# Differential attention scores: the low pass of q on half the array's rows, and both components of a query block scored in one step

## The chip, the cores and the metric

The kernel runs on one core of a Trainium2 chip. The metric is the device time of one execution in microseconds (us), lower is better; the time before is the median of three runs.

The core has a matrix engine (TensorE, PE; its weight loads are listed apart as PEld), a vector engine (VectorE, DVE), an engine for activations and copies (ScalarE, ACT), a general engine (GpSimd, POOL), and SyncE (SP), which issues the DMAs here. Each works through its own queue in order; semaphores join them. Matmul results land in PSUM.

## The reference

Two layers on 1024 tokens of width 1024: a pooling mixer and a gated MLP, then differential attention and a gated MLP. Attention has 8 heads; each has two components of 64 dimensions. Cut to what matters:

```python
def _diff_attention(x, w_qkv, ..., cos, sin, layer_idx):
    q, k, v = jnp.split(x @ w_qkv, 3, axis=-1)
    q = _rope(...).reshape(b, s, h, 2, dh) * (dh ** -0.5)      # h = 8 heads, 2 components, dh = 64
    k = _rope(...).reshape(b, s, h, 2, dh)
    v = v.reshape(b, s, h, 2 * dh)
    ...
    def one_block(qb):                                          # 128 queries
        sc = jnp.einsum('bqhce,bkhce->bhcqk', qb, k)
        p = jax.nn.softmax(sc, axis=-1)
        a = p[:, :, 0] - lam * p[:, :, 1]                       # component 0 minus lam times component 1
        return jnp.einsum('bhqk,bkhe->bqhe', a, v)
    o = lax.map(one_block, q_blocks)
    ...
    return _rms_norm(o, subln) * (1.0 - lam_init) @ w_o
```

All is float32 in the reference.

## The kernel before

Matmuls take 32-bit operands that are rounded. To keep precision, an operand is split into a high part (the rounded value) and a low part (what is left), and a product is computed as a sum of two or three matmuls.

**Layout of the scores.** The contraction of one component is 64 long, half of the 128 rows of the array. The tile `kst[:, c]` holds, for component c, the high part of k in rows 64c to 64c+63 (`own`) and its low part in the other 64 rows. q stands twice, in both halves: `qhi` is its high part, `qlo` its low part. So a matmul of `qhi[:, c]` with `kst[:, c]` over all 128 rows gives q_high x k_high + q_high x k_low, and the pass with `qlo[:, c]` gives q_low x k_high + q_low x k_low. A query block has 128 queries and 1024 keys, hence two matmuls of 512 columns for each pass and component.

**A query block**, 8 to a head, 64 in all. `score_q` makes `qhi` on ACT and `qlo` on POOL. `score_mm` runs the four matmuls of one component into a PSUM tile `sc` of 1024 columns (there are two such tiles), then DVE takes the row maximum (`nm`, L1108), for component 0 it subtracts a constant (L1110), and ACT takes the exponential and its row sum (L1111). `combine` (DVE, L1117 to L1122) forms component 0 minus the scaled component 1 in place, in two halves of the keys. `a_prep` transposes one half of the keys on PE (`aT`, L1137), and splits the result into `a_hi` (ACT) and `a_lo` (DVE, line 132 in a helper). `pv` multiplies two blocks at a time with v (`po`, L1148, 24 matmuls of 256 columns). `o_turn` transposes the output; `finish_*` normalizes a head.

**The order on PE** is written by hand: under `manual_schedule` PE executes in the order of the code, and the code is emitted by walking a string for each block, in turn the first and the second of `PLAN` (`PLAN7` in the last head). Each character is a step: `s` scores component 0 of this block, `S` component 1, `a` and `b` transpose the two halves of the block before, `q` is `score_q` of the next block, `c` is `combine`, `p` is `pv`, `t` is `o_turn`, and `.` takes the next step of `filler`: two matmuls of the projections of the next head (`pj`, L1020 and L1062), later of the output projection. On DVE, ACT and POOL the scheduler of the framework orders instructions by priority and by when it believes them ready.

Of the kernel before, what the change touches and what calls it, by code (L numbers as in the profile page):

```python
# [11 lines left out]
F32 = mybir.dt.float32  # L12
F32R = mybir.dt.float32r
I32 = mybir.dt.int32
AF = mybir.ActivationFunctionType
ALU = mybir.AluOpType
AX = mybir.AxisListType
# [3 lines left out]
P = 128  # L21
S = 1024
# [3 lines left out]
NT = S // P  # L26
NK = D // P
ORDER = (0, 4, 1, 5, 2, 6, 3, 7)
PLAN = ("...saq.bS..c.p", "st.aS.m.q.fb....F.c..")
PLAN7 = (".as.b....S.pqc.", "tmsaSqcb..f......F..")  # L30
AHEAD = 3
WQ, RQ = 14, 3
PB = (2, 1)
# [56 lines left out]
def trunk_kernel(  # L90
# [24 lines left out]
    V, A, PE = nc.vector, nc.scalar, nc.tensor  # L115

    def pool(es, name, bufs=1, space=None, side=None):
        kw = {}
        if space is not None:
            kw["space"] = space  # L120
        if side is not None:
            kw["side"] = side
        if space is not DRAM:
            kw["reuse_waits"] = "tile"
        return es.enter_context(tc.tile_pool(name=name, bufs=bufs, **kw))
# [824 lines left out]
    p_p = pool(at_es, "pp", bufs=2)  # L950
    a_p = pool(at_es, "ap", bufs=1)
    o_p = pool(at_es, "op", bufs=1)
    ps_sc = pool(at_es, "ps_sc", bufs=2, space=PSUM)
# [6 lines left out]
    for src, dst in ((cosT, cosF), (sinT, sinF)):  # L960
        wide = p_p.tile([P, NT, 4, 32], F32, name="prob0")
        V.tensor_copy(wide, src.unsqueeze(2).broadcast_to([P, NT, 4, 32]))
        for q in range(2):
# [3 lines left out]
            cols = slice(512 * q, 512 * q + 512)  # L967
# [109 lines left out]
    soft, sums = {}, {}  # L1077

    scored = {}

    def score_q(j, i):
        with tc.high_priority(offset=20):
            tq = qt[j, i // 2] if i % 2 == 0 else qt.pop((j, i // 2))
            src = tq[:, :, (i % 2) * P:(i % 2 + 1) * P]
            qhi = p_p.tile([P, 2, P], F32R, name="q_hi")
            qlo = p_p.tile([P, 2, P], F32R, name="q_lo")
            A.copy(qhi, src)  # L1087
            nc.gpsimd.tensor_tensor(qlo, src, f32(qhi), ALU.subtract)  # L1088
            scored[j, i] = qhi, qlo

    def score_mm(j, i, c):
        with tc.high_priority(offset=20):
            ks = kst[j]
            qhi, qlo = scored[j, i]
            if i == 0 and c == 0:
                sums[j] = p_p.tile([P, 2, NT], F32, name="sums")
            sm = sums[j]
            if c == 0:
                soft[j, i] = []
            soft[j, i].append(p_p.tile([P, S], F32, name=f"prob{c}", bufs=PB[c]))  # L1100
            if True:
                sc = ps_sc.tile([P, S], F32, name="sc")
                for l in (qhi, qlo):
                    for n in range(2):
                        ns_ = slice(n * 512, (n + 1) * 512)
                        PE.matmul(sc[:, ns_], l[:, c], ks[:, c, ns_], start=(l is qhi), stop=(l is qlo))  # L1106
                nm = small.tile([P, 1], F32, name=f"nm{c}")
                V.tensor_reduce(nm, sc, AX.X, ALU.max, negate=True)  # L1108
                if c == 0:
                    V.tensor_scalar(nm, nm, -10.0 * math.log(2.0), None, ALU.add)  # L1110
                A.activation(soft[j, i][c], sc, AF.Exp, bias=nm, accum_out=sm[:, c, i:i + 1])  # L1111

    def combine(j, i):
        with tc.high_priority(offset=50):
            (p0, p1), sm = soft[j, i], sums[j]
            r1 = small.tile([P, 1], F32, name="r1")
            V.reciprocal(r1, sm[:, 1, i:i + 1])  # L1117
            cc = small.tile([P, 1], F32, name="cc")
            V.scalar_tensor_tensor(cc, sm[:, 0, i:i + 1], neglam, r1, ALU.mult, ALU.mult)
            for q in range(2):  # L1120
                hq = slice(512 * q, 512 * q + 512)
                V.scalar_tensor_tensor(p0[:, hq], p1[:, hq], cc, p0[:, hq], ALU.mult, ALU.add)  # L1122
# [5 lines left out]
    def a_prep(j, i, q):  # L1128
        with tc.high_priority(offset=20):
            if i % 2 == 0 and q == 0:  # L1130
                at[j, i // 2] = (a_p.tile([P, NT, 256], F32R, name="a_hi"), a_p.tile([P, NT, 256], F32R, name="a_lo"))
            ahi, alo = at[j, i // 2]
            a = soft[j, i][0] if q == 0 else soft.pop((j, i))[0]
            pt = ps_tr.tile([P, 4, P], F32, name="aT", tag="tr")
            for k in range(4):
                kt = 4 * q + k
                PE.transpose(pt[:, k], a[:, kt * P:(kt + 1) * P], ident)  # L1137
            dsl = (slice(None), slice(4 * q, 4 * q + 4), slice((i % 2) * P, (i % 2 + 1) * P))
            split(pt, ahi[dsl], alo[dsl])

    def pv(j, pair):
        vhi, vlo = vst[j]
        ahi, alo = at.pop((j, pair))
        po = ps_tr.tile([P, 256], F32, name="po", tag="tr")
        n = 0
        for k in range(NT):
            for l, r in ((vhi, ahi), (vhi, alo), (vlo, ahi)):
                PE.matmul(po, l[:, k], r[:, k], start=(n == 0), stop=(n == 3 * NT - 1))  # L1148
                n += 1
        pos[j, pair] = po  # L1150
# [133 lines left out]

    assert sum(p.count('.') for p in PLAN) == 18
    done = []
# [4 lines left out]
    with tc.manual_schedule(engines={mybir.EngineType.PE}):  # L1291
        for g in range(H * NT + 2):
            j, i = divmod(g, NT)
            pj, pi = divmod(g - 1, NT)
            for step in (PLAN7 if j == H - 1 else PLAN)[g % 2]:
                if step == ".":
                    if j < H:
                        next(fill, None)
                elif step in "sS":
                    if j < H:  # L1300
                        score_mm(j, i, "sS".index(step))
                elif step == "q":
                    if g + 1 < H * NT:
                        score_q(*divmod(g + 1, NT))
                elif step == "c":
                    if j < H:
                        combine(j, i)
                elif step in "ab":
                    if 0 < g <= H * NT:
                        a_prep(pj, pi, "ab".index(step))  # L1310
                elif step == "p":
                    if 0 < g <= H * NT:
                        pv(pj, pi // 2)
                elif step == "t":
                    if g > 2:
                        hj, hi_ = divmod(g - 2, NT)
                        o_turn(hj, hi_ // 2)
                        if hi_ == NT - 1:
                            finish_a(hj)
                elif step == "m":  # L1320
                    if i == 3 and j:
                        finish_m(j - 1)
                        done.append(j)
                elif step in "fF":
                    if i == 3 and j:
                        finish_b(j - 1, "fF".index(step))
                        done.append(j)
# [85 lines left out]
```

## Time and profile before

| | |
|---|---|
| median of 3 runs | 2119.53 us (2117.35 to 2125.2) |
| profiled execution | 2117.11 us, span of its instructions 2115.3 us |
| mean granted TensorE clock | 0.98 |
| busy: PE / DVE / ACT / POOL | 2015.5 / 1558.6 / 1020.1 / 899.8 us |
| scores: first to last matmul | 803.9 to 1369.5 us of the span |
| score matmuls (512 columns) | 256 high and 256 low |
| row maxima on DVE, L1108 | 128, 155.7 us |
| exponentials on ACT, L1111 | 128, 142.7 us |

Times of instructions are from one profiled execution. An engine's busy time counts the stretches in which it had an instruction in hand; PE's matmul records overlap, so their durations do not add up. A row of the trace reads: start, duration, engine, line, operation, output <- inputs, shape, count.

### The profile page before, as it was taken

What the parts mean: (1) busy time and instruction counts of PE and PEld (TensorE: products, weight loads), DVE (VectorE), ACT (ScalarE), POOL (GpSimd) and SP (SyncE); (2) the same over time, 40 slices, a digit from 0 to 9 for tenths busy, and PEclk for the clock granted to TensorE, in tenths of its full rate; (3) what the DMA queues carried; (4) which work ended last, traced back from release to release, by engine and by line L of the source; (5) the groups of instructions that cost most, each with busy time, mean ns of one, the idle gap of its engine ahead of it and who ended that gap; (6) DMA issues with size and microseconds to landing.
All of it is one profiled execution on the core that took longest, in us unless ns stands there. A gap on an engine that the chain in (4) does not pass through costs nothing.

```text
span 2115.3 us, 27608 instructions
## 1 busy us (share of the span) xinstructions
PE 2015.5 (95%) x9659; PEld 1669.5 (79%) x9659; DVE 1558.6 (74%) x2278; ACT 1020.1 (48%) x1830; POOL 899.8 (43%) x689
## 2 busy tenths in 40 slices
PE   6789999999999799999999998987999999999997
PEld 5678888888888677888888887876888888888885
DVE  7867777777584648899889987767667777774646
ACT  7643333333453545676667666555433333344433
POOL 4599999995000000101110111024999999920000
PEclk8899999999999999999999999998999999999999
DMA  4225454554965412122212216253346445467653
GB/s 168 95 84 181 138 190 138 158 177 144 375 211 174 163 54 67 48 72 62 61 46 73 57 40 224 90 189 110 120 144 198 146 161 167 139 227 278 205 201 130
DMA packets 221720, 301.90 MB, mean 143 GB/s; under 512 B 17852, under 2 KB 142092, under 8 KB 218764
## 3 DMA queue, kind: packets, MB, share of 16 engines
q1 hardware_dynamic: 221580, 300.13, 43.4%
q8 instruction: 76, 1.25, 0.2%
q14 instruction: 64, 0.52, 0.1%
HBM read 196.78 MB, written 90.70 MB: 136 GB/s over the span
## 4 chain that ended last, share of the span: by engine, by line
PE 82%; DVE 9%; ACT 3%; DMA 3%; issue 2%; SPq 1%; POOL 0%; DVEq 0%; ACTq 0%; POOLq 0%
PE dn L597 17%; PE up_b L422 16%; PE up_c L422 11%; PE up_a L422 11%; PE pj L1020 6%; PE sc L1106 4%; PE pj L1062 4%; PE po L1148 3%; PE aT L1137 2%; PE pj L1233 2%; DVE nm L1108 1%; PE pp L844 1%; PE pl L824 1%; ACT hnT_hi L580 1%; DVE hnT_lo L581 1%
## 5 line engine op out<-in xcount | busy, mean ns | idle before, releaser
L1088 POOL TENSOR_TENSOR q_lo<-qt,q_hi 128x256 fp32r<-128x256 f32 x64 | 49.7, 777 | 698.3 <-ACT q_hi L1087 616.8
L380 POOL TENSOR_TENSOR w_lo<-s,w_hi 128x512 fp32r<-128x512 f32 x168 | 274.2, 1632 | 17.7 <-ACT w_hi L379 17.2
L597 PE MATMUL dn<-hnT_hi 128*128 128x512 f32 x584 | 229.7, 393 | 12.0 <-ACT hnT_hi L580 11.8
L597 PE MATMUL dn<-hnT_lo,hnT_hi 128*128 128x512 f32 x584 | 230.2, 394 | 4.4 <-DVE hnT_lo L581 4.4
L597 PE MATMUL dn<-hnT_hi,hnT_lo 128*128 128x512 f32 x584 | 228.8, 392 | 0.0
L422 PE MATMUL up_b<-x_hi,w_hi 128*128 128x512 f32 x528 | 207.2, 392 | 5.3 <-ACT x_hi L304 4.4
L422 PE MATMUL up_b<-x_lo,w_hi 128*128 128x512 f32 x528 | 206.6, 391 | 2.3 <-DVE x_lo L305 2.3
L380 POOL TENSOR_TENSOR w_lo<-raw,w_hi 128x512 fp32r<-128x512 f32 x130 | 195.3, 1503 | 30.6 <-ACT w_hi L379 26.4
L422 PE MATMUL up_b<-x_hi,w_lo 128*128 128x512 f32 x528 | 206.2, 391 | 0.0
L379 ACT CAST w_hi<-s 128x512 fp32r<-128x512 f32 x176 | 108.4, 616 | 178.9 <-PE up_b L422 87.4
L1108 DVE TENSOR_REDUCE nm<-sc 128x1 f32<-128x1024 f32 x128 | 155.7, 1216 | 15.4 <-PE sc L1106 14.6
L1111 ACT ACTIVATE prob<-sc,nm 128x1024 f32<-128x1024 f32 x128 | 142.7, 1115 | 22.3 <-DVE nm L1108 11.7
L422 PE MATMUL up_a<-hnT_hi,w_hi 128*128 128x512 f32 x352 | 139.3, 396 | 1.4 <-ACT g L499 0.9
L597 PEld LDWEIGHTS dn<-hnT_hi 128*128 128x128 f32 x584 | 110.5, 189 | 37.1 <-ACT hnT_hi L580 13.5
L422 PE MATMUL up_a<-hnT_lo,w_hi 128*128 128x512 f32 x352 | 138.9, 395 | 0.1
L422 PE MATMUL up_a<-hnT_hi,w_lo 128*128 128x512 f32 x352 | 138.5, 394 | 0.0
L394 POOL TENSOR_TENSOR s<-raw 128x512 f32<-128x512 f32 x84 | 133.1, 1584 | 10.3 <-DMA raw<-in_ffn_w_up_dram 4.1
L422 PE MATMUL up_c<-hnT_hi,w_lo 128*128 128x512 f32 x352 | 137.0, 389 | 0.2 <-DVE w_lo L380 0.2
L422 PE MATMUL up_c<-hnT_hi,w_hi 128*128 128x512 f32 x352 | 136.9, 389 | 0.0
L422 PE MATMUL up_c<-hnT_lo,w_hi 128*128 128x512 f32 x352 | 136.9, 389 | 0.0
L581 DVE TENSOR_TENSOR hnT_lo<-mst,hnT_hi 128x1024 fp32r<-128x1024 f32 (+1 forms) x80 | 90.2, 1127 | 61.3 <-ACT hnT_hi L580 61.1
L597 PEld LDWEIGHTS dn<-hnT_lo,hnT_hi 128*128 128x128 f32 x584 | 110.5, 189 | 31.0 <-DVE hnT_lo L581 8.4
(298 smaller groups left out, 5362.6 us busy)
## 6 DMA issues: line engine op xcount, KB each, us to landing
raw<-in_ffn_w_up_dram SPq DMA_DIRECT2D x88, 512.0 KB, 4.3
mst<-m_dram SPq DMA_DIRECT2D x70, 512.0 KB, 5.8
wd<-in_ffn_w_down_dram SPq DMA_DIRECT2D x22, 1024.0 KB, 6.0
wd_dram<-wd SPq DMA_DIRECT2D x22, 1024.0 KB, 6.4
m_dram<-cm SPq DMA_DIRECT2D x80, 256.0 KB, 5.6
wst<-wd_dram SPq DMA_DIRECT2D x40, 512.0 KB, 4.8
m_dram<-gc SPq DMA_DIRECT2D x66, 256.0 KB, 6.3
wst<-in_ffn_w_down_dram SPq DMA_DIRECT2D x30, 512.0 KB, 6.1
```

The costliest lines, as they stand in the source:

```text
L379: A.copy(hi, src)
L380: eng.tensor_tensor(lo, src, f32(hi), ALU.subtract)
L394: eng.tensor_tensor(t, a, b, op)
L422: PE.matmul(acc, l[a][:, k], r[b][:, k], start=first and n == 0, stop=n == 11, skip_group_check=True)
L581: V.tensor_tensor(l_, x, f32(h_), ALU.subtract)
L597: PE.matmul(banks[t], l[:, q, cols], r[:, q], start=first and cnt == 0, stop=stop and cnt == 3 * n - 1, skip_group_check=True)
L1020: PE.matmul(acc, l[:, k % 2, h], r[:, k], start=(n == 0), stop=(n == 3 * NK - 1))
L1062: PE.matmul(acc, l[:, k % 4], r[:, k], start=(n == 0), stop=(n == 3 * NK - 1))
L1106: PE.matmul(sc[:, ns_], l[:, c], ks[:, c, ns_], start=(l is qhi), stop=(l is qlo))
L1108: V.tensor_reduce(nm, sc, AX.X, ALU.max, negate=True)
L1111: A.activation(soft[j, i][c], sc, AF.Exp, bias=nm, accum_out=sm[:, c, i:i + 1])
L1148: PE.matmul(po, l[:, k], r[:, k], start=(n == 0), stop=(n == 3 * NT - 1))
```

## The change

`score_mm` now scores both components of a block at the step `s`; the step `S` is gone from the strings, in which nothing else changes. The four high matmuls (two for each component) come first, over 128 rows as before. Then the four low ones, each over only the 64 rows in which k's high part of its component stands: rows 0 to 63 for component 0, rows 64 to 127 for component 1, in turn, so that two neighbours lie on different halves of the array and write to different score tiles. The product q_low x k_low is no longer formed. The row maxima, the exponentials, their tiles and buffers are as before.

```diff
-PLAN = ("...saq.bS..c.p", "st.aS.m.q.fb....F.c..")
+PLAN = ("...saq.b..c.p", "st.a.m.q.fb....F.c..")
...
-    def score_mm(j, i, c):
+    def score_mm(j, i):
         with tc.high_priority(offset=20):
             ks = kst[j]
-            qhi, qlo = scored[j, i]
-            if i == 0 and c == 0:
+            qhi, qlo = scored.pop((j, i))
+            if i == 0:
                 sums[j] = p_p.tile([P, 2, NT], F32, name="sums")
             sm = sums[j]
-            if c == 0:
-                soft[j, i] = []
-            soft[j, i].append(p_p.tile([P, S], F32, name=f"prob{c}", bufs=PB[c]))
-            if True:
-                sc = ps_sc.tile([P, S], F32, name="sc")
-                for l in (qhi, qlo):
-                    for n in range(2):
-                        ns_ = slice(n * 512, (n + 1) * 512)
-                        PE.matmul(sc[:, ns_], l[:, c], ks[:, c, ns_], start=(l is qhi), stop=(l is qlo))
+            soft[j, i] = [p_p.tile([P, S], F32, name=f"prob{c}", bufs=PB[c]) for c in range(2)]
+            scs = [ps_sc.tile([P, S], F32, name="sc") for _ in range(2)]
+            cols = [slice(n * 512, (n + 1) * 512) for n in range(2)]
+            for c in range(2):
+                for ns_ in cols:
+                    PE.matmul(scs[c][:, ns_], qhi[:, c], ks[:, c, ns_], start=True, stop=False)
+            for ns_ in cols:
+                for c in range(2):
+                    own = slice(64 * c, 64 * c + 64)
+                    PE.matmul(scs[c][:, ns_], qlo[own, c], ks[own, c, ns_], start=False, stop=True)
+            for c in range(2):
                 nm = small.tile([P, 1], F32, name=f"nm{c}")
-                V.tensor_reduce(nm, sc, AX.X, ALU.max, negate=True)
+                V.tensor_reduce(nm, scs[c], AX.X, ALU.max, negate=True)
                 if c == 0:
                     V.tensor_scalar(nm, nm, -10.0 * math.log(2.0), None, ALU.add)
-                A.activation(soft[j, i][c], sc, AF.Exp, bias=nm, accum_out=sm[:, c, i:i + 1])
+                A.activation(soft[j, i][c], scs[c], AF.Exp, bias=nm, accum_out=sm[:, c, i:i + 1])
...
-                elif step in "sS":
+                elif step == "s":
                     if j < H:
-                        score_mm(j, i, "sS".index(step))
+                        score_mm(j, i)
```

The lines of the changed kernel are numbered two higher from the exponentials on; its high score matmuls are L1103, its low ones L1107, the row maxima L1110, the constant L1112, the exponentials L1113, the transposes L1139.

What moves is seen on two engines at one place, the third block of the fourth head. PE before; `prob_9217` is the combined tile of the block before, `hnT_*` the normalized input of the projections:

```order
L1106 MATMUL sc<-kst,q_hi 128x512 x2
L1106 MATMUL sc<-kst,q_lo 128x512 x2
L1137 MATMUL aT<-ident,prob_9217 128x128 x4
L1020 MATMUL pj<-hnT_hi_69,wq_hi 128x512
L1020 MATMUL pj<-hnT_hi_69,wq_lo 128x512
L1137 MATMUL aT<-ident,prob_9217 128x128 x4
L1106 MATMUL sc<-kst,q_hi 128x512 x2
L1106 MATMUL sc<-kst,q_lo 128x512 x2
L1020 MATMUL pj<-hnT_lo_70,wq_hi 128x512
```

PE after, the same place:

```order
L1103 MATMUL sc<-kst,q_hi 128x512 x4
L1107 MATMUL sc<-kst,q_lo 128x512 x4
L1139 MATMUL aT<-ident,prob_9217 128x128 x4
L1020 MATMUL pj<-hnT_hi_69,wq_hi 128x512
L1020 MATMUL pj<-hnT_hi_69,wq_lo 128x512
L1139 MATMUL aT<-ident,prob_9217 128x128 x4
L1020 MATMUL pj<-hnT_lo_70,wq_hi 128x512
```

The four matmuls of component 1 have moved up to those of component 0, past eight transposes and two projection matmuls. (The order prints an output's rows, 128; that the low ones contract over 64 rows it does not show.)

DVE before, the same block; `t_*` are the rotary products of the next head's projection:

```order
L1029 TENSOR_TENSOR t_9283<-t_9283,t_9331 128x512
L1108 TENSOR_REDUCE nm_9364<-sc 128x1
L132 TENSOR_TENSOR a_lo<-aT,a_hi 128x4x128
L1110 TENSOR_SCALAR nm_9364<-nm_9364 128x1
L1108 TENSOR_REDUCE nm_9395<-sc 128x1
L132 TENSOR_TENSOR a_lo<-aT,a_hi 128x4x128
L1049 TENSOR_TENSOR kst<-kf,kst 64x512
L1117 RECIPROCAL r_9402<-sums 128x1
```

DVE after:

```order
L1029 TENSOR_TENSOR t_9283<-t_9283,t_9331 128x512
L1110 TENSOR_REDUCE nm_9370<-sc 128x1
L132 TENSOR_TENSOR a_lo<-aT,a_hi 128x4x128 x2
L1112 TENSOR_SCALAR nm_9370<-nm_9370 128x1
L1110 TENSOR_REDUCE nm_9374<-sc 128x1
L1049 TENSOR_TENSOR kst<-kf,kst 64x512
L1119 RECIPROCAL r_9402<-sums 128x1
```

The second `a_lo` has moved ahead of the constant of component 0 and of the maximum of component 1.

More of the change, by code (lines that the diff above doesn't have):

```diff
@@ L28 @@
 ORDER = (0, 4, 1, 5, 2, 6, 3, 7)
-PLAN = ("...saq.bS..c.p", "st.aS.m.q.fb....F.c..")
-PLAN7 = (".as.b....S.pqc.", "tmsaSqcb..f......F..")
+PLAN = ("...saq.b..c.p", "st.a.m.q.fb....F.c..")
+PLAN7 = (".as.b.....pqc.", "tmsaqcb..f......F..")
 AHEAD = 3
```

## The prediction

> **What bounds the kernel now.** I read the page first, for the engine that is busy all the time and for the end chain, then the attention stage by windows, then who waits for whom there, and last single matmuls in order of time.
>
> ```profile
> span 2115.3 us, 27608 instructions
> ...
> PE 2015.5 (95%) x9659; PEld 1669.5 (79%) x9659; DVE 1558.6 (74%) x2278; ACT 1020.1 (48%) x1830; POOL 899.8 (43%) x689
> ...
> PE   6789999999999799999999998987999999999997
> DVE  7867777777584648899889987767667777774646
> ...
> PE 82%; DVE 9%; ACT 3%; DMA 3%; issue 2%; SPq 1%; POOL 0%; DVEq 0%; ACTq 0%; POOLq 0%
> ```
>
> TensorE (PE) is busy 95% of the span, and 82% of the chain that ended last is on it. Attention lies in slices 16 to 26. PE is at 9 there in all but one, VectorE (DVE) at 8 and 9 in all but the last two, its highest for so long. The middle of that stage, all engines first and the row maxima (L1108) alone second:
>
> ```profile
> 870.00:1290.00 420.00, 417.04 (x2339) 351.37 (x2338) 375.33 (x725) 276.82 (x619) 63.37 (x126) 1.00 0.21 59
> ```
> ```profile
> 870.00:1290.00 420.00, 115.82 (x96) 1.00 0.21 59
> ```
>
> Columns are length, busy time of PE, weight loads, DVE, ScalarE (ACT), POOL, then granted clock, DMA share and GB/s. There are two maxima to a query block, so 48 blocks pass in 420 us, 8.75 us each. PE is busy 417 of 420 at full clock. DVE is busy 375/48 = 7.82 us a block, 0.93 less than the block lasts. So PE sets the pace, and what PE saves here moves everything behind it. DVE would stop a saving only beyond 0.93 us a block. What PE waits for in the whole stage, in us, times, longest:
>
> ```profile
> PEld sc L1106 <- ACT prob L1111: 1.6, 1, 1.6
> PE sc L1106 <- ACT prob L1111: 1.2, 1, 1.2
> PE aT L1137 <- DVE r L1168: 3.0, 6, 0.5
> PE aT L1137 <- DVE prob L1122: 2.8, 2, 2.0
> ```
>
> That is 8.6 us in 64 blocks, 0.13 each at most.
>
> **The change part by part.** (a) The matmuls. Their number stays:
>
> ```profile
> L1106 PE MATMUL sc<-kst,q_hi x256: 387/395/776, 804.2 to 1369.0; 128*128 128x512 f32 x128
> L1106 PE MATMUL sc<-kst,q_lo x256: 387/393/632, 804.6 to 1369.5; 128*128 128x512 f32 x128
> ```
>
> 256 low ones over 64 blocks are four a block. They keep 512 columns, but each fills only 64 rows of the array, and two neighbours fill different halves. Nothing is removed; a gain exists only if two halves run at once. One scoring and what follows it, matmuls and then weight loads:
>
> ```profile
> 1014.42 0.63 PE L1106 MATMUL sc<-kst,q_hi 128*128 128x512 f32 x2
> 1014.89 0.62 PE L1106 MATMUL sc<-kst,q_lo 128*128 128x512 f32 x2
> 1015.35 0.60 PE L1137 MATMUL aT<-ident,prob 128*128 128x128 f32 x4
> 1015.70 0.48 PE L1020 MATMUL pj<-hnT_hi,wq_hi 128*128 128x512 f32 x1
> 1016.02 0.39 PE L1020 MATMUL pj<-hnT_hi,wq_lo 128*128 128x512 f32 x1
> ```
> ```profile
> 1014.66 0.42 PEld L1106 LDWEIGHTS sc<-kst,q_lo 128*128 128x128 f32 x2
> 1015.12 0.59 PEld L1137 LDWEIGHTS aT<-ident,prob 128*128 128x128 f32 x4
> 1015.68 0.19 PEld L1020 LDWEIGHTS pj<-hnT_hi,wq_hi 128*128 128x128 f32 x1
> 1015.79 0.19 PEld L1020 LDWEIGHTS pj<-hnT_hi,wq_lo 128*128 128x128 f32 x1
> ```
>
> Two things are to be seen. Four matmuls go from 1014.42 to 1015.35, so one costs 0.2325 us, though its record lasts 0.39: the other 0.16 us is the tail in the array and PSUM, over which the next one already runs. And each has its own load, issued when the matmul before it starts; where matmuls are short the loads set the pace, 0.11 us apart (1015.68, 1015.79, and the three steps from 1015.35 to 1015.68).
>
> No row here has two matmuls on different rows at once, so I bound the four low matmuls, now 4 x 0.2325 = 0.93 us. Upper end: no overlap, 0.93, saves nothing. Lower end: both halves entirely together, 2 x 0.2325 = 0.465, saves 0.465. I take the value that the load row gives. With loads 0.11 apart the pairs start at 0, 0.11, 0.2325 and 0.3425, and the last ends at 0.575. That saves **0.355 us a block**, 22.7 us in 64.
>
> The Trainium skill, "TensorE: Matmul & The Clock Gate", section "Measured speedup vs the span model", gives a pack of row tiles the duration of one matmul plus about 4 ns a tile; by it the saving would be nearly the 0.465. No run here shows it yet.
>
> (b) The switch. PE goes from whole-array matmuls to half-array ones and back once a block, so 64 times each way. Call the cost of one switch x. The nearest row is the step from matmul to transposes and back at 1015.35 and 1015.70: beyond the load pace of 0.11 it costs nothing, so x can be 0. At the other end the array runs empty, which is the tail of 0.16, and then loads uncovered, 0.11: x = 0.27. A negative x is excluded, since a switch does no work. I take one uncovered load for the two switches together, **0.11 us a block**, 7.0 us in 64, nearer to the transposes' row because that is also a change of mode between matmuls of this stage.
>
> The Trainium skill, "TensorEngine Tiling (Array Packing)", section "Key Properties", says that changing the tiling mode, not just the tile, drains TensorE. That speaks against the change. If the drain is the 0.16 tail on both sides, it takes 0.32 of the 0.355, and the sum would be about zero instead of this gain; the transposes here show no drain, but they keep the 128 rows.
>
> (c) Both components together. The second scoring moves up to the first, past one half of the transposes, a projection step and the other half. DVE and ACT do the same instructions. What changes is when: PE now needs both score buffers free within 0.465 us of each other, and both maxima arrive together. The tightest place I found is a block whose DVE queue has four rotary products ahead of the maxima (the third of the fourth head):
>
> ```profile
> 1031.51 0.69 DVE L1026 TENSOR_TENSOR t<-pj,cosF 128x512 f32<-128x512 f32 x1 [0.62 <-PE pj L1020]
> ...
> 1033.93 1.21 DVE L1108 TENSOR_REDUCE nm<-sc 128x1 f32<-128x1024 f32 x1
> 1035.07 0.67 DVE L132 TENSOR_TENSOR a_lo<-aT,a_hi 128x512 fp32r<-128x512 f32 x1
> 1035.66 0.14 DVE L1110 TENSOR_SCALAR nm<-nm 128x1 f32<-128x1 f32 x1
> 1035.72 1.21 DVE L1108 TENSOR_REDUCE nm<-sc 128x1 f32<-128x1024 f32 x1
> ...
> 1039.14 1.41 DVE L1122 SCALAR_TENSOR_TENSOR prob<-prob,cc,prob 128x512 f32<-128x512 f32 x2
> ```
> ```profile
> 1035.84 1.12 ACT L1111 ACTIVATE prob<-sc,nm 128x1024 f32<-128x1024 f32 x1 [1.17 <-DVE nm L1110]
> 1036.85 0.19 ACT L1111 ACTIVATION_READ_ACCUMULATOR prob<-sc,nm 128x1 f32 x1
> 1036.94 0.60 ACT L1048 CAST kst<-kf 64x512 fp32r<-64x512 f32 x1
> 1037.45 1.11 ACT L1111 ACTIVATE prob<-sc,nm 128x1024 f32<-128x1024 f32 x1
> ```
> ```profile
> 1031.31 0.62 PE L1106 MATMUL sc<-kst,q_hi 128*128 128x512 f32 x2
> ...
> 1038.99 0.63 PE L1106 MATMUL sc<-kst,q_hi 128*128 128x512 f32 x2
> ...
> 1040.61 0.60 PE L1137 MATMUL aT<-ident,prob 128*128 128x128 f32 x4
> ```
>
> In the new order both a_lo stand ahead of the TENSOR_SCALAR, 0.59 us more. The first exp then starts at 1036.43, the cast 1.10 later, the second exp at 1038.04 and ends at 1039.15. The next scoring would come at 1038.99 - 0.355 = 1038.64, its second component 0.465 later at 1039.10: PE waits 0.05. The combination starts 1.69 after the second exp starts (1037.45 to 1039.14), so at 1039.73; its first half, 0.75, ends at 1040.5. The transposes that read it come 1.62 after the scoring before, and 0.575 more now that the scoring is longer, at 1040.83. So the long way still fits by 0.3 us. The tightest place is just met, others have more room. Behind a late scoring stand, on PE, the transposes of the block before and the projections, and ACT's a_hi casts wait for those. Ends of this term: the present 0.13 us of waits goes away, since the combination has a scoring's worth more time; or one of the two kinds of tight block in each head is late by a whole maximum and exp, 1.21 + 1.11, on two places a head, 16 x 2.32 = 37 us, 0.58 a block. I take **0.05 us a block lost**, 3.2 us, the wait of the row above. What the queues carry otherwise (q_lo on POOL, all DMAs) is not moved past anything on PE: the low parts are needed four matmuls after the high ones instead of two, which is later, not earlier.
>
> Sum a block: -0.355 + 0.11 + 0.05 = -0.195 us, times 64 = -12.5 us. Against the profiled execution's own 2117.1 us that is 2104.6; the median of the three runs, 2119.5, lies 2.4 above that execution, so 2107.
>
> **The rivals.** In general the change is 64 x (-s + 2x + 0.05), with s the overlap saved.
> - *The switch eats it* (x = 0.16, the tail twice): 64 x 0.015 = +1 us, 2120.5. For it: half-array rows change where sums leave the array, and each matmul has the tail. Against: the transposes' row.
> - *Slower: the array empties and then loads* (x = 0.27): 64 x (-0.355 + 0.54 + 0.05) = +15 us, 2134.5. It decides for slower by over 0.5% from x = 0.235 on. For it: a load that needs the half of the array that is still running can't go ahead; against: every load in the rows above goes ahead of a running matmul.
> - *The halves do not overlap*, so the change doesn't do what it says: s = 0, x = 0 to 0.11: +3 to +17 us, 2123 to 2137. For it: PE starts matmuls one after another in all rows here. Against: nothing in the trace, since nothing tries.
> - *The waits grow*: with w in place of 0.05, the gain is gone at w = 0.245, some 16 us of PE waiting for exps. DVE has 0.93 a block to spare, so I count this into the width.
>
> **How the numbers follow.** Within 0.5% (10.6 us, about what runs of this kernel can tell) means 2109 to 2130. Overlap with x up to 0.11: 0.47, of which 0.41 ends faster and 0.06 within. The switch eats it: 0.24, within. No overlap: 0.16, of which 0.07 within and 0.09 slower. Empties and loads: 0.13, slower. So faster 0.41, same 0.37, slower 0.22. The likeliest gives 2107, with its own range 2095 (x = 0 and loads that overlap more, toward s = 0.465: 64 x -0.415 = -27 at the extreme) to 2114 (x = 0.11). The whole range has to take in the drain and most of no overlap: 2095 to 2131.
>
> **What would show it.** In the trace after: the starts of the low matmuls of a pair 0.1 us or less apart, not 0.23, show overlap; the time from the last high matmul to the first low one, and from the last low one to the transpose behind it, gives x directly. PE waiting for prob at the scores shows term (c). 48 blocks should take about 411 us in place of 420, with DVE's busy time as it is. Wrong would be: starts 0.23 apart (no overlap), a gap of 0.2 or more at each switch, or PE waits for exps over 10 us.

## The result

The changed kernel takes 2139.35 us (median of 5 runs, 2136.02 to 2142.8) against 2122.9 (5 runs, 2117.35 to 2125.2) of the kernel before beside it: ratio 1.0084, 95% interval 1.0062 to 1.0105. It is 16 us slower, where 12 us less had been forecast, and outside the range. Its profiled execution took 2142.0 us. From the page of the kernel after:

```profile
span 2140.1 us, 27626 instructions
...
PE 2020.7 (94%) x9659; PEld 1641.8 (77%) x9659; DVE 1559.5 (73%) x2278; ACT 1023.9 (48%) x1830; POOL 907.9 (42%) x689
...
PE 76%; DVE 13%; ACT 4%; issue 3%; DMA 2%; POOL 2%; SPq 0%; DVEq 0%; ACTq 0%; POOLq 0%
```

PE's share of the chain that ended last fell from 82% to 76%, DVE's rose from 9% to 13%. The same 420 us by windows (length, busy PE, weight loads, DVE, ACT, POOL):

```profile
870.00:1290.00 420.00, 405.81 (x2275) 319.26 (x2273) 362.63 (x708) 273.37 (x605) 68.21 (x124) 0.99 0.20 55
```

PE, which was idle for 3 us here, is now idle for 14, and fewer instructions fit (2275 matmul records, 2339 before). The starts of the heads (first score matmul of each, in us of the span, then the first matmul of the second layer's up projection; attention is the time between the first and the last of these) tell in which part of the program the time lies. The last two rows are experiments told below. (In the table of the kernel before, 803.9 is the first score's weight load.)

| kernel | 1st head | 2nd | 3rd | 7th | 8th | up | attention |
|---|---|---|---|---|---|---|---|
| before | 804.2 | 873.6 | 944.0 | 1225.7 | 1294.3 | 1458.2 | 654.0 |
| after | 809.2 | 881.5 | 953.3 | 1243.0 | 1314.9 | 1482.7 | 673.6 |
| e1, full low pass | 804.3 | 875.0 | 948.4 | 1239.7 | 1310.9 | 1477.6 | 673.3 |
| e15, pairs in 55 blocks | 804.6 | 873.7 | 943.3 | 1223.6 | 1292.2 | 1455.1 | 650.5 |

Attention grew by 19.6 us. The 5 us ahead of it are the execution's, not the change's: the kernel before with two steps moved (e13) began its scores at 810.1. From the up projection to the end of the last matmul it takes 645.2 to 646.4 us in every kernel here but one (e7, 647.6).

**The halves do overlap, and the switches cost.** One scoring of the kernel after and what follows it, matmuls and then weight loads:

```profile
1032.75 1.07 PE L1103 MATMUL sc<-kst,q_hi 128*128 128x512 f32 x4
1033.74 0.73 PE L1107 MATMUL sc<-kst,q_lo 64*128 64x512 f32 x4
1034.41 0.44 PE L1168 MATMUL oT<-ident,oc 128*128 128x128 f32 x2
```
```profile
1033.74 0.30 PEld L1107 LDWEIGHTS sc<-kst,q_lo 64*128 64x128 f32 x4 [0.35 <-issue]
1034.40 0.20 PEld L1168 LDWEIGHTS oT<-ident,oc 128*128 128x128 f32 x2 [0.36 <-ACT q_hi L1087]
```

The four low matmuls take 0.67 us to the next operation in place of 0.93. One by one, they start at 1033.744, 1033.747, 1034.079 and 1034.081: the two of a pair 2 to 3 ns apart, so the halves run wholly together and 0.465 is saved. But the last high matmul starts at 1033.426 and the first low one 0.318 later, the pairs are 0.335 apart, and 0.325 lies between the last pair and the transposes, where 0.2325 was the pace; the loads at both edges are no longer hidden (0.35 and 0.36 idle ahead of them). That is 0.28 us over the pace. Another 0.06 lies just behind: the second transposition starts 0.164 after the first, where in the kernel before the same step took 0.108.

**PE now waits for DVE.** The largest waits of PE and of DVE on POOL in attention (804 to 1400 us; total, times, longest):

```profile
PEld sc L1107 <- issue: 22.7, 62, 0.7
PEld po L1150 <- DVE a_lo L132: 20.0, 18, 2.3
...
PE po L1150 <- DVE a_lo L132: 12.8, 15, 1.9
...
DVE rr L1188 <- POOL rs_y L168: 10.3, 7, 3.1
...
PEld sc L1103 <- ACT prob L1113: 5.8, 7, 2.8
```

The first row is the switch, 62 times 0.37. The second and third are what is new: `po`, the product with v, waits for `a_lo`. In the kernel before (804 to 1375 us) these waits were almost nothing, but they were there:

```profile
PEld po L1148 <- DVE nm L1110: 2.5, 8, 0.8
...
PEld po L1148 <- DVE a_lo L132: 1.3, 7, 0.2
```

All but one of these stand in the third blocks of the heads, two weight loads of some 0.2 us in most; the matmuls themselves waited once, 0.4 us. So `po` came there just as its input was ready, with next to no room. Now the wait is in the first block of a head (0.3 us) and above all in the third. In the five inner heads the third block grew from 7.69 us to 9.45 (10.78 in the last of them) and the first from 7.42 to 7.75, and where PE did not wait the blocks shrank by about 0.1: the second from 9.46 to 9.34, the sixth from 9.45 to 9.38, the seventh from 7.41 to 7.34, the eighth from 10.33 to 10.23. Of the 0.465 there is 0.1 left, so the two switches take 0.36; the steps above hold 0.34 of it. The third block of the fourth head, PE, then DVE:

```profile
1046.32 0.40 PE L1020 MATMUL pj<-hnT_hi,wq_lo 128*128 128x512 f32 x1
1048.59 0.39 PE L1150 MATMUL po<-a_hi,v_hi 128*128 128x256 f32 x1 [1.87 <-DVE a_lo L132]
```
```profile
1042.70 0.17 DVE L1188 SCALAR_TENSOR_TENSOR rr<-vo,rs_y 128x8 f32<-128x8 f32 x1 [1.20 <-POOL rs_y L168]
...
1043.10 0.69 DVE L1026 TENSOR_TENSOR t<-pj,cosF 128x512 f32<-128x512 f32 x1
...
1044.31 1.34 DVE L1030 TENSOR_TENSOR t<-t,t 128x512 f32<-128x512 f32 x1
1045.58 1.22 DVE L1029 TENSOR_TENSOR t<-t,t 128x512 f32<-128x512 f32 x1
1046.72 1.21 DVE L1110 TENSOR_REDUCE nm<-sc 128x1 f32<-128x1024 f32 x1
1047.86 1.27 DVE L132 TENSOR_TENSOR a_lo<-aT,a_hi 128x512 fp32r<-128x512 f32 x2
```

The scoring began at 1042.09; its first maximum comes 4.63 us later, against 2.62 before (1033.93 after 1031.31). Two things stand ahead of it. DVE waits 1.20 us for `rr`, the scale of the head that has just ended, which needs POOL's reciprocal root. And the products L1030 and L1029 take 1.34 and 1.22 instead of 0.69 and 0.68, as they did before:

```profile
1030.54 0.14 DVE L1186 SCALAR_TENSOR_TENSOR rr<-vo,rs_y 128x8 f32<-128x8 f32 x1
...
1032.71 0.69 DVE L1030 TENSOR_TENSOR t<-t,t 128x512 f32<-128x512 f32 x1
1033.33 0.68 DVE L1029 TENSOR_TENSOR t<-t,t 128x512 f32<-128x512 f32 x1
```

POOL's rows, after and then before, show what ran beside them:

```profile
1038.48 0.20 POOL L164 TENSOR_TENSOR rs_a<-rs_y,rs_c 128x8 f32<-128x8 f32 x1 [3.09 <-DVE rs_y L161]
...
1042.46 0.20 POOL L168 TENSOR_TENSOR rs_y<-rs_a,rs_y 128x8 f32<-128x8 f32 x1
1043.21 1.90 POOL L1190 TENSOR_TENSOR oq<-oq,rr 128x1024 f32<-128x1024 f32 x1 [0.55 <-DVE rr L1189]
1045.06 1.19 POOL L1088 TENSOR_TENSOR q_lo<-qt,q_hi 128x256 fp32r<-128x256 f32 x1
```
```profile
1025.32 0.20 POOL L164 TENSOR_TENSOR rs_a<-rs_y,rs_c 128x8 f32<-128x8 f32 x1 [6.67 <-DVE rs_y L161]
...
1028.44 0.20 POOL L168 TENSOR_TENSOR rs_y<-rs_a,rs_y 128x8 f32<-128x8 f32 x1
...
1030.96 1.90 POOL L1188 TENSOR_TENSOR oq<-oq,rr 128x1024 f32<-128x1024 f32 x1 [1.63 <-DVE rr L1187]
```

The root takes twelve small POOL instructions. In the second block of a head DVE now has both maxima ahead of the values that start it (before, only the first), so it starts 5.73 us after that block's scoring (1032.75) in place of 3.47 (1021.85), and ends inside the third block's work. In the kernel before, `rr` came at 1030.54 without a wait, and POOL's product with `oq` (to 1032.86) had only 0.15 us left when L1030 began at 1032.71.

### The profile page after: what moved, and what is told of

It is laid out like the page before. It is cut to its first block, busy times and chain, and to the rows that moved or that the text cites. A ratio compares the mean times of both kernels' runs of the same rounds, so it can differ in the third digit from the quotient of the medians.

```text
span 2140.1 us, 27626 instructions
## 1 busy us (share of the span) xinstructions
PE 2020.7 (94%) x9659; PEld 1641.8 (77%) x9659; DVE 1559.5 (73%) x2278; ACT 1023.9 (48%) x1830; POOL 907.9 (42%) x689
## 4 chain that ended last, share of the span: by engine, by line
PE 76%; DVE 13%; ACT 4%; issue 3%; DMA 2%; POOL 2%; SPq 0%; DVEq 0%; ACTq 0%; POOLq 0%
PE dn L597 17%; PE up_b L422 16%; PE up_c L422 11%; PE up_a L422 11%; PE po L1150 4%; PE pj L1062 4%; PE pj L1020 4%; DVE nm L1110 3%; PE sc L1103 2%; PE sc L1107 2%; PE pj L1235 1%; PE aT L1139 1%; PE pp L844 1%; DVE a_lo L132 1%; PE pl L824 1%
## 5 line engine op out<-in xcount | busy, mean ns | idle before, releaser
L1110 DVE TENSOR_REDUCE nm<-sc 128x1 f32<-128x1024 f32 x128 | 152.2, 1216 | 28.0 <-PE sc L1107 27.1
L1113 ACT ACTIVATE prob<-sc,nm 128x1024 f32<-128x1024 f32 x128 | 142.1, 1113 | 42.9 <-DVE nm L1112 29.0
```

The costliest lines, as they stand in the source:

```text
L1110: V.tensor_reduce(nm, scs[c], AX.X, ALU.max, negate=True)
L1113: A.activation(soft[j, i][c], scs[c], AF.Exp, bias=nm, accum_out=sm[:, c, i:i + 1])
```

## The experiments

Theory W: the pairs gain about 0.1 us a block, and scoring both components together loses more through the order on DVE, ACT and POOL. Rival S: the switches cost what was lost. Theories M, B and D came up later and are named where they are first tested. The kernel before, run beside each set, had medians from 2122.3 to 2123.2.

**e1: both together, but no half-array.**

```diff
-                    PE.matmul(scs[c][:, ns_], qlo[own, c], ks[own, c, ns_], start=False, stop=True)
+                    PE.matmul(scs[c][:, ns_], qlo[:, c], ks[:, c, ns_], start=False, stop=True)
```

> Both components scored together as in the kernel after, but the low pass over all 128 rows again, so no half-array and no switch; VectorE's order is that of the kernel after. Theory W (the half-array pairs gain a little on TensorE, and the loss comes from what scoring both together does to the order of VectorE, ScalarE and GpSimd): the pairs net 0.465 - 2 x 0.18 = about 0.1 us a block, so this is 0 to 8 us slower than the kernel after, 2139 to 2147, and still has the 2 us wait for a_lo ahead of po in the third block of each head. Rival S (the two switches of array shape in each block cost the time): the loss goes with the switches, 2118 to 2128, as the kernel before.

2141.65 us, ratio 1.0093 (1.0076 to 1.011): as slow as the kernel after, without a single switch. Attention takes 673.3 us against 654.0. Its waits:

```profile
PEld po L1149 <- DVE a_lo L132: 18.4, 18, 2.2
...
DVE rr L1187 <- POOL rs_y L168: 8.1, 7, 1.2
```

Both rows are there as in the kernel after. So rival S falls: scoring both together costs 19.3/64 = 0.30 us a block by itself. The kernel after takes 673.6 in attention with its pairs, so by these two executions they gained nothing on the whole.

**e2: the half-array alone, with each component scored for itself.**

```diff
                     for n in range(2):
                         ns_ = slice(n * 512, (n + 1) * 512)
-                        PE.matmul(sc[:, ns_], l[:, c], ks[:, c, ns_], start=(l is qhi), stop=(l is qlo))
+                        own = slice(0, P) if l is qhi else slice(64 * c, 64 * c + 64)
+                        PE.matmul(sc[:, ns_], l[own, c], ks[own, c, ns_], start=(l is qhi), stop=(l is qlo))
```

> The kernel before, each component scored for itself at its own place, only that its two low matmuls run on the 64 rows of their own component, as in the kernel after: four switches in a block, nothing overlapped, VectorE's order that of before. Theory W with a switch of 0.16 to 0.20 us: 4 x 64 x 0.18 = +46, 2160 to 2175. With the switch as forecast (0.055): +14, about 2137. Rival S, in which the whole loss of the kernel after is switches (0.465 saved, 0.26 lost net, so 0.36 a switch): 4 x 64 x 0.36 = +92, about 2215.

2163.21 us, ratio 1.0189 (1.017 to 1.0209). Attention takes 696.7 us, 42.7 more than before, for 256 switches: 0.167 us each. A scoring of one component, matmuls and loads:

```profile
1187.46 0.61 PE L1107 MATMUL sc<-kst,q_hi 128*128 128x512 f32 x2
1188.01 0.73 PE L1107 MATMUL sc<-kst,q_lo 64*128 64x512 f32 x2
1188.67 0.66 PE L1138 MATMUL aT<-ident,prob 128*128 128x128 f32 x4
```
```profile
1188.01 0.29 PEld L1107 LDWEIGHTS sc<-kst,q_lo 64*128 64x128 f32 x2 [0.35 <-issue]
1188.66 0.42 PEld L1138 LDWEIGHTS aT<-ident,prob 128*128 128x128 f32 x4 [0.36 <-issue]
```

From the first matmul to the transposes 1.21 us, where the kernel before had 0.93 (1014.42 to 1015.35). Each switch shows the same idle 0.35 as in the kernel after. The 0.167 is an average: the second, sixth and eighth block grew by 0.74 to 0.76, which is 0.19 a switch, and the fourth, in which PE waited before, by only 0.21.

The Trainium skill, "TensorEngine Tiling (Array Packing)", section "Key Properties", says that changing the mode drains TensorE; it gives no size. These runs show a price that agrees with it, 0.167 us a switch over the stage and 0.19 in blocks without waits.

**e3: the low matmuls in the order component 0, 0, 1, 1.**

```diff
-            for ns_ in cols:
-                for c in range(2):
-                    own = slice(64 * c, 64 * c + 64)
+            for c in range(2):
+                own = slice(64 * c, 64 * c + 64)
+                for ns_ in cols:
                     PE.matmul(scs[c][:, ns_], qlo[own, c], ks[own, c, ns_], start=False, stop=True)
```

> The kernel after with the four low matmuls of a block in the order component 0, 0, 1, 1 in place of 0, 1, 0, 1: only the middle two stand on different halves next to each other. If halves overlap as the trace of after shows (pair starts 2 to 3 ns apart, the next pair 0.228 later), the run takes three slots of 0.23 in place of two: up to 64 x 0.23 = +15 over the kernel after, 2145 to 2155, less where TensorE waits anyway. With the overlap as forecast (loads at 0.11): +7. No overlap at all: +0.

2142.85 us, ratio 1.0099 (1.0081 to 1.0118), not told apart from the kernel after. The 15 us did not come: blocks in which PE does not wait are as long (the second 9.32 against 9.34, the eighth 10.24 against 10.23). In one scoring the four start at 1022.896, 1022.903, 1023.233 and 1023.238, still in pairs, 5 to 7 ns apart in place of 2 to 4. In 62 of the 64 scorings the two late ones carry the semaphore updates that end a component's sum; in the program as built these are the second and the fourth. So the third started ahead of the second, whose half was busy.

**e4: `rr` behind the first maximum of the third block** (`red` keeps the instruction of each maximum).

```diff
+        with tc.issue_after(red[min(j + 1, H - 1), 2 if j < H - 1 else NT - 1, 0]):
-        V.scalar_tensor_tensor(rr, v, 3.0e38, y, ALU.is_lt, ALU.mult)
+            V.scalar_tensor_tensor(rr, v, 3.0e38, y, ALU.is_lt, ALU.mult)
```

> The kernel after with one move on VectorE: the two small rr products that close a head's output scale are queued behind the first maximum of the next head's third block, in place of ahead of its four rotary products, where they wait 1.2 us for GpSimd. Theory W: the 2 us wait ahead of po in the third block goes, 7 heads x 1.8 = 12 us less than the kernel after, 2125 to 2130. Rival S: no change, 2136 to 2142.

2139.96 us, ratio 1.0085 (1.0069 to 1.01): no change, which is what rival S said, for another reason. The third block fell from 9.45 to 7.97 us as theory W wanted, and the fourth rose from 10.9 to 12.45. DVE, POOL and PE in the same head:

```profile
1050.07 0.15 DVE L1191 SCALAR_TENSOR_TENSOR rr<-vo,rs_y 128x8 f32<-128x8 f32 x1
...
1050.80 2.15 DVE L1049 TENSOR_TENSOR kst<-kf,kst 64x512 fp32r<-64x512 f32 x1 [0.37 <-ACT kst L1048]
```
```profile
1050.51 1.90 POOL L1193 TENSOR_TENSOR oq<-oq,rr 128x1024 f32<-128x1024 f32 x1 [4.42 <-DVE rr L1192]
```
```profile
1058.24 0.66 PE L1141 MATMUL aT<-ident,prob 128*128 128x128 f32 x4 [1.53 <-DVE nm L1114]
```

`rr` got in only behind the second maximum; POOL's product then fell beside the split of k (2.15 us, 0.69 elsewhere), the combination came late, and the fourth block's transposes waited. Theory W's 2125 to 2130 was missed.

**e5: `rr` right behind the rotary products.** As e4, with `issue_after` on L1029 of that block and a high priority for both `rr`. Rival M, new here, is that both maxima ahead of `a_lo` cost the time wherever `rr` stands.

> The kernel after with the rr products queued right behind the four rotary products of the next head's third block, one place earlier than in e4 (there they came behind the second maximum, and GpSimd's product, and the key split beside it, came so late that the fourth block grew by 1.55 us as the third shrank by 1.5). Theory W (order of VectorE): the wait ahead of po in the third block goes and the fourth block keeps its 10.9: 7 x 1.5 = 10 us less than the kernel after, 2126 to 2132. Rival M (both maxima of a block ahead of its a_lo cost the time wherever the rr stand): 2136 to 2142 again, with the wait moved on.

2131.65 us, ratio 1.0039 (1.0025 to 1.0054): 8 us of the loss gone, with the third block at 8.12 and the fourth at 10.41. PE's matmuls still wait 0.5 us for `a_lo` there, and now 0.4 in the seventh (7.94 us, 7.34 in the kernel after). Theory W is half right, and so is M.

**e6 and e7: the maxima apart.** Component 1's maximum is queued behind the first `a_lo` (`with tc.issue_after(last[0])`, the instruction that made it); e6 has e5's `rr` too.

> As e5, and VectorE's maxima apart as in the kernel before: first maximum, first a_lo, second maximum, second a_lo. TensorE's order is that of the kernel after. Theory W, with rival M: all waits of the kernel after are order on VectorE, so what is left is TensorE's own gain of about 0.1 us a block: 2113 to 2120. A third theory, B (scoring both components at once holds both score buffers, and the exponentials come too late for the next block whatever the order): 2128 to 2140.

> The kernel after with the maxima apart on VectorE (first maximum, first a_lo, second maximum, second a_lo), the rr products where the scheduler then puts them, in the second block ahead of the combine. Theory M: the gain of e6, 2113 to 2122. Theory W of the rr alone: no change or worse, 2136 to 2145, since rr then wait for GpSimd ahead of the combine in the second block.

e6: 2131.32 us, ratio 1.0045 (1.0028 to 1.0062), as e5: the first block is clean (7.35), but the second `a_lo` is now late behind the second maximum, the third block takes 8.93, the fifth 8.46 and the eighth 11.04. M's 2113 to 2120 is refuted. The time is in theory B's range, but not by B's way: between 880 and 1240 us PE's loads wait for maxima and `a_lo` ahead of `po` (7.7 and 7.1 us) and for `a_lo` ahead of the transposes of v (5.2), not for exponentials ahead of scores. e7: 2153.23 us, ratio 1.0144 (1.0127 to 1.0161), worse than any theory had it:

```profile
1041.68 0.17 DVE L1199 SCALAR_TENSOR_TENSOR rr<-vo,rs_y 128x8 f32<-128x8 f32 x1 [1.04 <-POOL rs_y L168]
```

Here the scheduler put `rr` in the second block, between the maxima and the combination, and the third block took 12.25 us (11.1 in the later heads). Between e6 and e7, which differ in the place of these two instructions of 0.17 us alone, lie 22 us.

**e8: e7 with the full low pass.**

> e7 with the low pass over all 128 rows: both components scored together, no half-array. It prices the half-array pairs with the waits gone: if a switch is 0.17 and the overlap 0.465 a block, it is 64 x 0.12 = 8 us slower than e7. Under the forecast of the prediction (0.355 saved, 0.11 for both switches) 64 x 0.245 = 16 us slower. If the pairs gain nothing: the same as e7.

2154.42 us, ratio 1.0157 (1.0138 to 1.0177). It is 1.2 us above e7, not the 8 of the forecast, and so prices nothing; that the pairs' gain goes into the wait where PE waits is the likely reason.

**e9, e10, e11: fill steps moved ahead of `po`.** Theory D: the second scoring used to lie between the transposes and `po`, 0.93 us of PE's work that covered `a_lo`; two projection steps can take its place. e9 is the kernel after, e10 the kernel before, e11 is e9 with the full low pass.

```diff
-PLAN = ("...saq.b..c.p", ...
+PLAN = (".saq.b....c.p", ...
```

> The kernel after with two of the three fill steps ahead of the even blocks' scoring moved between the second group of transposes and po: PLAN's even row is .saq.b....c.p in place of ...saq.b..c.p. Theory D (scoring both together took 0.93 us of TensorE work away from between the transposes and po, and put the second maximum ahead of a_lo, so po waits for a_lo): two fill steps give the 0.93 back, and VectorE's order changes with it (the rr products now stand ahead of the maxima while scoring still runs, and the rotary products behind): the waits of the even blocks go, and TensorE's own gain is left: 2112 to 2122. Rival M (the order of VectorE as a whole is too tight for both maxima at once, so the wait moves on, as in e4 and e6): 2128 to 2140.

> The kernel before with the same two fill steps moved, its scoring as it was. It tells what the move does without the change. Theory D: before has no wait at po to remove, so nothing is won, 2120 to 2130; rival: the move is worth something by itself, under 2118, and then a gain of e9 isn't the change's.

> e9 with the low pass over all 128 rows, VectorE's order that of e9: it prices the half-array pairs where TensorE waits least. With 0.465 saved and two switches of 0.17: 64 x 0.12 = 8 us slower than e9. By the forecast of the prediction (0.355 and 0.11 for both switches): 16 us slower. With the overlap kept and a switch of 0.23, or with the waits still in charge: the same as e9.

e9: 2131.91 us, ratio 1.0047 (1.0032 to 1.0062); e10: 2130.63, 1.0034 (1.0021 to 1.0046); e11: 2134.64, 1.0052 (1.0034 to 1.007). In e9 every wait at `po` in the inner heads is gone, and a new one stands in the first block, now 10.52 us:

```profile
953.16 0.66 PE L1139 MATMUL aT<-ident,prob 128*128 128x128 f32 x4 [1.59 <-DVE nm L1112]
```
```profile
950.15 2.35 DVE L1110 TENSOR_REDUCE nm<-sc 128x1 f32<-128x1024 f32 x2
952.42 0.68 DVE L132 TENSOR_TENSOR a_lo<-aT,a_hi 128x512 fp32r<-128x512 f32 x1
```

The transposition of v (`v_turn`) now falls between the two groups of transposes, and the second group has to wait for one of the two transpose buffers until DVE, behind both maxima, has read it. e10 loses in the same block (9.77 in place of 7.42 plus 0.93), so this is the move's price and not the change's. Rival M's range was met, with another cause. e11 is 2.7 us above e9, within the spread of either, not the 8 expected.

**e12, e13, e14: the same move in the third, fifth and seventh block only.**

```diff
+PLAN_LATE = ".saq.b....c.p"
...
-            for step in (PLAN7 if j == H - 1 else PLAN)[g % 2]:
+            for step in (PLAN7[g % 2] if j == H - 1 else PLAN_LATE if i in (2, 4, 6) else PLAN[g % 2]):
```

> e9 with the two fill steps moved in the third, fifth and seventh block of a head only; the first block keeps the row of the kernel after, so that the v turn doesn't fall between its two groups of transposes. Theory D (waits for a_lo and rr are all of the loss): the periods of a head are those of e9 but for the first block, which falls from 10.52 to about 8.3 in e9's count: 7 to 8 heads x 2 us less than e9, 2112 to 2120, below the kernel before. Rival M (a further limit): 2126 to 2135, with the 2 us found in another block.

> The kernel before with the same move as e12. Theory D: e10 lost 1.4 us in each first block and 8 in all, which go with the first block's row put back: 2118 to 2124, no gain of its own, so that e12's gain against it is the change's: 64 x 0.11 = 7. Rival: the move itself wins, under 2115.

> e12 with the low pass over all 128 rows, VectorE's order that of e12: both together, no half-array. With 0.465 saved and two switches of 0.17 to 0.18: 64 x 0.11 = 7 us slower than e12. By the prediction's terms (0.355 and 0.11): 16 us slower. With the waits still in charge: 0 to 3.

e12: 2122.79 us, ratio 1.0001 (0.9992 to 1.001): the whole loss is gone, though theory D's 2112 to 2120 is missed. e13: 2124.05, 1.0004 (0.9994 to 1.0014), so the move by itself wins nothing in the kernel before. e14: 2123.87, 1.0005 (0.9994 to 1.0016), not the 7 us above e12. e12's waits at `po` and its 420 us:

```profile
PEld po L1151 <- DVE a_lo L133: 3.8, 7, 0.6
```
```profile
870.00:1290.00 420.00, 414.20 (x2348) 327.55 (x2347) 368.96 (x735) 283.61 (x624) 66.24 (x126) 1.00 0.22 60
```

20.0 us of waits became 3.8, and in 420 us there are more matmuls than in the kernel before (2348, 2339). The clean blocks price the pairs: second block 8.40 in e12 against 8.51 in e14, sixth 8.43 and 8.54, seventh 8.27 and 8.36, so 0.09 to 0.11 a block. Little of it reached the total: attention takes 656.7 us in e12 and 660.2 in e14, and the medians are 1.1 apart. The fifth block gains nothing: from the second head on it takes 8.6 to 9.8 us in both kernels (8.3 and 8.4 in the first head), and on average 0.1 longer in e12. Its transposes wait there for DVE's part of the finished head's transposed output (`oTs`), in e12 and then in e14:

```profile
PE aT L1140 <- DVE oTs L133: 4.1, 6, 1.2
```
```profile
PE aT L1139 <- DVE oTs L133: 2.7, 3, 1.2
```

And e12 loses at the ends, where its first and last heads take 71.7 and 166.5 us against 69.4 and 163.9 before. There the fill steps are few or empty, so probably nothing covers two maxima in a row.

**e15 and e16: the pairs where they pay.** e12 with the kernel before's scoring in the first block of the first head and in the last head; e16 is e15 with the full low pass. `score_one` is the `score_mm` of the kernel before.

```diff
-                elif step == "s":
-                    if j < H:
+                elif step in "sS":
+                    apart = j == H - 1 or g == 0
+                    if j < H and apart:
+                        score_one(j, i, "sS".index(step))
+                    elif j < H and step == "s":
                         score_mm(j, i)
```

> e12, but the first block of the first head and all of the last head are scored as in the kernel before, one component at a time with the low pass over 128 rows; 55 of 64 blocks keep the pairs. Theory D: the first head's first block goes back by 1.7 us and the last head by 2.6: 4 us less than e12, 2116 to 2120, 0.1 to 0.3% below the kernel before. Rival: the ends give nothing back, 2121 to 2126.

> e15 with the low pass over 128 rows in its 55 blocks too: 55 x 0.10 (0.465 saved, two switches of 0.18) = 5.5 us slower than e15, 2121 to 2126. By the prediction's terms, 55 x 0.245 = 13 slower. With no worth in the pairs: the same.

e15: 2116.61 us, ratio 0.9979 (0.9965 to 0.9992), 0.2% below the kernel before. e16: 2121.74, 0.9998 (0.9987 to 1.0009). The two differ in the low pass alone, and their medians by 5.1 us; the spread of the twelve times of each allows 2 to 9. In the profiled executions attention takes 650.5 and 653.2 us, 2.7 apart; most of the rest of their difference lies ahead of attention (804.6 and 809.9), where the code is the same. So the pairs gain something on the whole kernel, 0.05 to 0.09 us for each of 55 blocks, while 0.1 in the clean ones is the firmer price. e15's 420 us:

```profile
870.00:1290.00 420.00, 414.69 (x2353) 328.14 (x2352) 366.92 (x728) 283.13 (x624) 66.05 (x126) 1.00 0.22 60
```

2353 matmuls, against 2339 before and 2275 in the kernel after.

## Why the prediction was wrong

- **Step (a), the overlap: right that it exists, under-sized.** It took s = 0.355, with the second of a pair starting a weight load later (0.11). The pairs start 2 to 4 ns apart, so s = 0.465, the lower end of its own bounds on the time.
- **Step (b), the switch: mis-sized by three.** It took 0.11 for both switches, one uncovered load, leaning on the step between matmuls and transposes, which shows no cost but keeps all 128 rows on both sides. e2 measures 0.167 to 0.19 a switch, and the pairs leave 0.09 to 0.11 of the 0.465, so 0.36 for two. The prediction had nearly the right value among its rivals (x = 0.16, the tail twice) and chose the wrong row to stand for it. (a) and (b) together are -0.10 a block where -0.245 was put: 9 us of the miss.
- **Step (c), the waits: this is the step that failed.** It put 0.05 us a block and e1 gives 0.30, 16 us of the miss. The prediction looked for the tightest place, found the right block (the third of a head) and followed two ways there, from the maximum to the score buffer and from the combination to the next transposes. Both held: at the scores PE's loads wait 5.8 us in all, and for the combination not at all. It did not follow the third way, `a_lo` to `po`, and its list of PE's waits, given as the whole stage, leaves out the two rows of `po` shown above, which had no room in this very block. The 0.93 us that DVE had to spare was an average over 48 blocks. The second scoring was work between the transposes and `po`; with it moved up, `po` came 0.93 us sooner after its transposes, while `a_lo` came later. It took DVE's start in that block from the trace of before (rotary products from 1031.51), though the two small `rr` ahead of them depend on a chain through POOL which the new order started 2.3 us later.
- **The rivals.** "The waits grow" was named, counted into the width and not given a chance; it turned out to be the case, at six times its size, and as waits for `a_lo` and not for exponentials. The upper end of (c), 0.58, would have held it. The slower rival (the array empties and loads) had the wrong place: e1 has no switch and is as slow.
- **What would show it.** The starts of a pair were to be 0.1 us or less apart: they are. A gap of 0.2 or more at each switch was to tell against it: at the edges there is only 0.09 over the pace, and 0.10 more lies between the two pairs and 0.06 behind the first transposition, where the prediction did not look. 48 blocks (the second head to the seventh) took 433 us, 421 before, where the forecast was 411 in place of 420. "PE waits for exps over 10 us" was the wrong sign to watch; they were waits for `a_lo`, 20 us.
- **The sum with the measured terms**: 64 x (-0.465 + 0.36 + 0.30) = +12.5 us; measured by the medians +16.5, with its interval from +13 to +22. Attention takes the same time with pairs and without (673.6, e1 673.3), so the 0.1 of the clean blocks did not come out in sum, which is the direction of the rest. The range's lower end is a little off too: 27 us less is 2093, not 2095.

That the loss is waits and not the pairs is shown by e1, e12 and e15: it is there without pairs, with fill steps ahead of `po` it goes, and e15 with pairs is below e16 without. Left open are why e3 was 6 us longer in attention than the kernel after in its profile while its clean blocks were equal, and why `oTs` comes late in more heads of e12 (six) than of e14 (three).

## What to carry to other kernels

When a step moves on the engine that sets the pace, list every wait on that engine behind it, with the slack of each in each kind of block, and not the tightest chain alone: the work that moves away was cover for something. A forecast for an in-order engine has to follow small instructions that depend on another engine too, since two of 0.17 us stood ahead of everything here. Packing halves of the array pays per visit: two pairs saved 0.465 us and two switches took 0.36, so try to collect more pairs between two switches before paying for them with the order of the other engines (no run here does).

## What the hardware showed that was not expected

- Matmuls on different halves start 2 to 4 ns apart, and in e3 a matmul whose half is free starts ahead of an earlier one whose half is busy. The Trainium skill, "TensorE: Matmul & The Clock Gate", section "The mechanism", has matmuls start strictly in program order; e3's semaphore updates say otherwise, unless the last step of the build swapped the two, which no trace shows.
- A DVE product with both inputs in SBUF seems to stand still until the POOL instruction beside it ends: L1030, L1029 and e4's L1049 end 0.54, 0.55 and 0.54 us after it (1045.65 after 1045.11, 1046.80 after 1046.25, 1052.95 after 1052.41); undisturbed they take 0.68 to 0.69. In attention of the kernel after, all 13 rotary products that began beside a longer POOL instruction ended 0.55 us behind it. L1026, with one input in PSUM, stays at 0.68 to 0.69 beside the same `oq`. The Trainium skill, "SBUF — State Buffer", section "SBUF: two separate sides", describes an exclusive lock on a shared pair of ports; these rows agree with it.
